# Five more Strassen steps at new places, SiLU in one instruction, and the opening's squares in PSUM

## The chip, the cores and the metric

The kernel runs on one core of a Trainium2 chip. The metric is the device time of one execution in microseconds (us), lower is better; several executions are timed and their median is given. Engines are named as the profile names them: PE is TensorE (PEld its weight loads), DVE is VectorE, ACT is ScalarE, POOL is GpSimd, SP is SyncE, which here only issues transfers.

## The reference

One decoder block in float32 on 256 tokens of width 4096: an RMSNorm, a wide projection, two mixer branches, gates, an output projection with a residual, and a final RMSNorm.

```python
h = rmsnorm(x, norm_w)
proj = einsum('bsd,de->bse', h, w_in)                  # 4096 -> 20480
u_p, z_p, u_c, b_c, c_c, z_c, g_logit = split(proj)    # 6 of width 2048, one of 8192
y_pool = causal_multiscale_pool(u_p, pool_w, pool_scale) * silu(z_p)
y_conv = causal_gated_shortconv(u_c, b_c, c_c, conv_w, conv_b) * silu(z_c)
br = einsum('bsnc,ncd->bsnd', stack(y_pool, y_conv), w_branch)
merged = sum(sigmoid(g_logit + gate_b) * br)           # over the two branches
x = x + einsum('bsd,de->bse', merged, w_out)
return rmsnorm(x, final_norm_w)
```

SiLU is z times its sigmoid. Nearly all the arithmetic is in the three large products (w_in, w_branch, w_out).

## The kernel before

**Units and steps.** The products are cut into units of 1024 output columns, named after what they compute: `cu0 cc0 cz0 cb0 cu1 cc1 cz1 cb1` (convolution branch), `pz0 pu0 pz1 pu1` (pooling branch), `g0_0 g1_0 ... g1_3` (gates), `b0_0 ... b1_3` (branch products), `o0 ... o3` (output). A unit has 16 steps (a branch unit 8). A step takes 256 rows of weights, loads them into one of four `raw` buffers (SP, the queue of `load`, L90), splits each float into a high and a low part in the `ring` buffer (high by ACT, L72; low by a subtraction on DVE, L75), and multiplies: each product of two floats is three matmuls of 128x512 (L1297): high by high, high by low, low by high.

**Two kinds of step.** A plain step ("P") makes 2 token halves x 2 column halves x 2 row halves x 3 = 24 matmuls. A Strassen step ("S") makes seven products in place of eight, so 21 matmuls, and pays for it with sums on DVE: two of the weights' blocks are combined (`W<-raw`, `raw<-raw,W`) and there are three parts to split, so DVE has six instructions where a P step has two. The sum of two of its weight blocks is made in DRAM: SP copies one block to `sum_d` (L1252), POOL adds the other to it with an accumulating transfer (`move_add`, L97), and SP loads the sum. `PLACES` and `OUT` name, for each unit, the step numbers (0 to 15) that are Strassen steps. The others are P. There are 216 S steps.

**Order.** Every engine runs its instructions in the order in which the program writes them. The program walks through PE's steps; after each group of matmuls `pump` writes the preparation of up to three steps ahead, as far as the ring has room, and once every six matmuls `tick` writes the next item of a queue: the epilogue of the unit just finished (one item in the queue is an action, `None` is a pause of one tick) and the filling of the standing operands. The epilogues of the z units (`cz0 cz1 pz0 pz1`) use `sigmoid_mul`:

```python
def sigmoid_mul():
    return gap(4) + [lambda: act(E, R, AF.Sigmoid)] + gap(1) + [lambda: mul(R, R, E)]
```

**The standing operands of the output units.** The products of the branch units, gated and merged, are transposed on PE in each b1 unit's epilogue (`transposes`, L519), copied to `Y`, stored to DRAM (`m_d`) and fetched again by SP into one of two staging tiles, `sa` and `sb`; from there they are split into `arena`. An operand of an S step needs sums first (`sums_s`, four DVE instructions `sa<-...`). `queue_fills` queues these fills in the order in which o0 will use them, that is, in the order that `OUT[0]` gives. The last b1 unit's epilogue lies in the first steps of o0: there DVE multiplies by the gates (`R<-R,E`) and adds the other branch (`R<-R,Y`) for each token half, and PE transposes R right after step 4 has begun.

**The opening.** In the first unit (all P steps) x is split as well, and its squares are summed for the norm, `square(c)` after the preparation of steps 2 to 9: ACT squares into the one tile `W`, DVE adds it to `sq` (the tile `sa`), twice per step. At step 10 PE sums over the partitions (L1086), ACT and DVE make the reciprocal root (`mean`, `rin`, `diag`), and at step 11 PE spreads it (L1094).

Of the kernel before, what the change touches and what calls it, by code (L numbers as in the profile page):

```python
# [29 lines left out]
AF = mybir.ActivationFunctionType  # L30
# [3 lines left out]
T = 256  # L34
# [23 lines left out]
def hybrid_block(ctx: ExitStack, tc: tile.TileContext, x, x_t, norm_t, w_first, w_in, pool_w, pool_scale,  # L58
# [12 lines left out]
    def act(dst, src, func=AF.Copy, **kw):  # L71
        return pin(nc.scalar.activation(dst, src, func, **kw))  # L72

    def tt(dst, a, b, op):
        return pin(nc.vector.tensor_tensor(out=dst, in0=a, in1=b, op=op))  # L75

    def mul(dst, a, b):
        return tt(dst, a, b, ALU.mult)

    def add(dst, a, b):  # L80
        return tt(dst, a, b, ALU.add)
# [23 lines left out]
    def sb(name, shape, dt=F32):  # L105
        return const.tile(shape, dt, name=name)
# [4 lines left out]
    R = sb("R", [P, 2, NU])  # L111
    E = sb("E", [P, 2, NU])
    W = sb("W", [P, NH])
# [45 lines left out]
    def xc(a, b=None):  # L159

        q = flat(xhome[a // 4])[:, a % 4 * 2 * T:((b or a + 1) - 1) % 4 * 2 * T + 2 * T]
        return q if b else q.rearrange("p (k c) -> p k c", k=2)
# [269 lines left out]
    SHARED = [("F", t, n) for t in range(2) for n in range(2)]  # L432
# [5 lines left out]
    def shared(i):  # L438
        return PF[i]
# [71 lines left out]
    def transposes(src, done):  # L511

        items = []
        for j in range(4):
            def f(j=j):
                for i in range(2):
                    for t in range(2):
                        c = (2 * j + i) * P
                        pin(nc.tensor.transpose(shared(j)[:, i * T + t * P:i * T + (t + 1) * P],  # L519
                                                src[:, t, c:c + P], ident))  # L520
                done(j)
            items.append(f)
        return items
# [16 lines left out]
    def gap(n):  # L540
        return [None] * n

    def sigmoid_mul():
        return gap(4) + [lambda: act(E, R, AF.Sigmoid)] + gap(1) + [lambda: mul(R, R, E)]

    units = []

# [61 lines left out]
    def at_places(at):  # L609
        n = NP_X + NS_X  # L610
        ps, ss = list(range(n - len(at))), list(range(n - len(at), n))
        return [("S", ss.pop(0)) if i in at else ("P", ps.pop(0)) for i in range(n)]
# [159 lines left out]
    def band_sums(st):  # L772
        c = st.band
        for b in range(8):
            g = b // 4
            o = shared(b // 2)[:, (b % 2) * T:(b % 2 + 1) * T]
            cs = slice(b * P, (b + 1) * P)
            bands, edge = upper["bands"], upper["edge"]
            pin(nc.tensor.matmul(o, st.h[:, 0, cs], bands[:, g], start=True, stop=False))  # L779
            pin(nc.tensor.matmul(o, st.l[:, 0, cs], bands[:, g], start=False, stop=False))  # L780
            pin(nc.tensor.matmul(o[:, P:T], st.h[:, 1, cs], edge[:, g], start=False, stop=False))
            pin(nc.tensor.matmul(o[:, P:T], st.l[:, 1, cs], edge[:, g], start=False, stop=True))
        rg.release(st.block, 16)
        e = chan(E)
        for i in range(2):
            w = WINDOWS[2 * c + i]
            for j in (2 * i, 2 * i + 1):
                act(e[:, 2 * j:2 * j + 2], bankview(j), scale=1.0 / w)
                mul(e[:, 2 * j:2 * j + 2, 0:w - 1], bankview(j)[:, :, 0:w - 1],
                    ic[:, None, 0:w - 1].to_broadcast([P, 2, w - 1]))  # L790
            st.unit.flags[f"pooled{i}"] = True

    def mix(st):
        g = st.g
        for t in range(2):
            o = shared(2 * g + t)
            ts = slice(t * P, (t + 1) * P)
            for k in range(4):
                for i, (a, b) in enumerate(((st.ah, st.h), (st.ah, st.l), (st.al, st.h))):
                    pin(nc.tensor.matmul(o, a[:, k, ts], b[:, k], start=(k, i) == (0, 0), stop=(k, i) == (3, 2)))  # L800
        rg.release(st.bw, 16)
        rg.release(st.ba, 8)
        cs = slice(g * NH, (g + 1) * NH)
        for t in range(2):
            mul(R[:, t, cs], shared(2 * g + t), Y[:, t, cs])
        if g == 1:
            c = st.c

            def copy(j):
                act(chan(E)[:, 2 * j:2 * j + 2], bankview(j))  # L810
            queue.extend(gap(3) + transposes(R, copy) + [e_done(2, 1), lambda: put(y_d[0, c], chan(E), QUEUE[9]), e_done(8)])
# [37 lines left out]
    merged = {}  # L849


    OUT = ((6, 7, 9, 11, 12, 13, 15), (2, 4, 5, 7, 8, 10, 11, 15), (2, 3, 4, 6, 10, 11, 12, 13), (1, 3, 5, 7, 9, 10, 12))

    def out_unit(c):
        cs = slice(c * NU, (c + 1) * NU)
# [11 lines left out]
        def src(i):  # L867
            return wout[c, i]
        seq = at_places(OUT[c])
        units.append(Unit(f"o{c}", src, seq, m_ops, epi, before=start))  # L870
# [82 lines left out]
    now, filled, units_done = [0], [0], [False]  # L953
# [115 lines left out]
    sq = sa.rearrange("p o c -> p (o c)")  # L1069

    def square(c):

        src = xc(2 * c, 2 * c + 2)
        if c == 0:
            act(sq, src, AF.Square)
        else:
            for n in range(2):
                act(W, src[:, n * 2 * T:(n + 1) * 2 * T], AF.Square)
                add(sq[:, n * 2 * T:(n + 1) * 2 * T], sq[:, n * 2 * T:(n + 1) * 2 * T], W)
        if c == 7:  # L1080
            for n in (2 * T, T):
                add(sq[:, 0:n], sq[:, 0:n], sq[:, n:2 * n])
# [119 lines left out]
    loaded = [s for s in steps if s.src is not None]  # L1202
    for i, s in enumerate(loaded):
        s.load_index = i
    state = dict(limit=0, nl=0, np=0, micros=None, prepared=0, now=0, mm=0)
    queue = deque()

    def issue_load(s):
# [94 lines left out]
    def after_group(u, b):  # L1303
        if b[0] == "E" and u is not last:
            if u.closed(b):
                evacuate(u, *b[1:])
        while state["mm"] >= TICK:
            state["mm"] -= TICK
            tick()
        state["limit"] = state["now"] + min(AHEAD, state["now"] + 1)  # L1310
        pump()
# [5 lines left out]
    def order_of(seq):  # L1317
        return [i for _, i in seq]

    def queue_fills():  # L1320
# [6 lines left out]
        def from_y(n, o, i, ready=None):  # L1327
            later(o, y_d[n, i // 4][:, i % 4].rearrange("p k t -> p (k t)"), place_of(o),
                  ready or (lambda: n == 0 or units_done[0]))

        def from_m(o, i):
            c = i // 4
            if c < 3:
                later(o, m_d[c][:, i % 4].rearrange("p k t -> p (k t)"), place_of(o),
                      lambda: c in merged and now[0] >= merged[c])
            else:
                def src():
                    return chan(Y)[:, 2 * (i % 4):2 * (i % 4) + 2].rearrange("p k (t c) -> p k t c", t=2)
                fills.append(Direct(o, src, place_of(o), lambda: 3 in merged))
# [4 lines left out]
        for n in DIRECT_LAST:  # L1344
            for i in range(NP_Y[n], ny):
                from_y(n, y_last[n][i], i, lambda: all(o.ready for q in y_ops for o in q))
        for i in order_of(at_places(OUT[0])):
            from_m(m_ops[i], i)

    def run_step(u, st):  # L1350
        if st.kind == "B":
            band_sums(st)
            state["mm"] += 10
            after_group(u, ("F", 0, 0))
            return
        if st.kind == "M":
            mix(st)
            state["mm"] += 24
            after_group(u, ("F", 0, 0))
            return  # L1360
        for f in st.first:
            f()
        while not st.op.ready:
            pop_fill(True)
        assert st.kind != "S" or st.op.kind == "S" or st.op.more
        gs = st.groups()
        for i, g in enumerate(gs):
            multiply(u, st, g)
            if i == len(gs) - 1:
                st.op.left -= 1  # L1370

            if st is not steps[0] or i >= len(gs) // 2 - 1:
                after_group(u, g[0])
            if st is steps[0] and i == len(gs) // 2 - 1:
                warm_up(WARM_2)
# [213 lines left out]
```

## Time and profile before

| | |
|---|---|
| median of 3 timed runs | 2369.02 us (2366.8 to 2370.43) |
| the profiled execution: device time | 2372.13 us |
| the profiled execution: span, first to last instruction | 2370.4 us |
| busy in that span: PE / DVE / ACT / POOL | 2350.2 / 2165.5 / 1448.8 / 250.8 us |
| matmuls of 128x512 at L1297 | 7497 in `sums`, 2556 in `shared` |
| HBM traffic | 324 GB/s over the span |

The profile is of one execution. A line of a timeline gives the start and the duration in us, the engine, the source line, the operation, output<-inputs, the shapes, how many instructions are merged in the line, and in brackets how long the engine had been idle before it and what ended that. A line of groups gives the count, then busy us and mean ns of one after the bar, then the idle time before. `SPq` is SP's queue, `PEld` weight loads. Busy matmuls overlap by a part of their length, so the distance of their starts is shorter than the duration of one.

### The profile page before, as it was taken

The numbers are of one execution on the slowest core, as the hardware profiler recorded it, in microseconds if no ns is written. First come the engines' busy times: TensorE is split into PE (matmuls) and PEld (weight loads), VectorE is DVE, ScalarE is ACT, GpSimd is POOL, SyncE is SP. The second block draws the span as 40 slices with busy tenths as digits, with TensorE's granted clock in tenths as the row PEclk, the third lists the DMA queues.
The fourth block names the chain that finished last, engine by engine and source line by source line (L and its number), as shares of the span: only waits on it lengthen the run. The fifth ranks groups of instructions, "written<-read, shape, count | busy, mean of one in ns | idle before, by whom it ended". The sixth has DMA issues, their size and how long they took to land.

```text
span 2370.4 us, 29327 instructions
## 1 busy us (share of the span) xinstructions
PE 2350.2 (99%) x10456; PEld 1943.0 (82%) x10456; DVE 2165.5 (91%) x2345; ACT 1448.8 (61%) x1708; POOL 250.8 (11%) x336
## 2 busy tenths in 40 slices
PE   9999999999999999999999999999999999999998
PEld 7788888888888888888888888888888888788886
DVE  7999999989889979989999999989899898798988
ACT  7655665656556656566665666666565556566555
POOL 0000111010012011110111111100000000111110
PEclk9999999999999999999999999999999999999999
DMA  9777998897998788789999999999988788799886
GB/s 337 228 252 240 299 304 263 280 288 219 299 303 276 244 269 285 227 283 278 306 305 293 307 299 309 276 295 296 305 288 270 269 289 282 243 272 330 270 284 245
DMA packets 178708, 664.06 MB, mean 280 GB/s; under 512 B 19952, under 2 KB 20208, under 8 KB 145024
## 3 DMA queue, kind: packets, MB, share of 16 engines
q1 hardware_dynamic: 135472, 549.28, 63.1%
q0 software_dynamic: 42656, 111.82, 24.1%
q8 instruction: 82, 1.34, 0.2%
q10 hardware_dynamic: 432, 1.07, 0.1%
q14 instruction: 66, 0.54, 0.1%
HBM read 629.26 MB, written 138.74 MB: 324 GB/s over the span
## 4 chain that ended last, share of the span: by engine, by line
PE 95%; DVE 2%; ACT 1%; DMA 1%; issue 1%; SPq 0%; DVEq 0%; ACTq 0%
PE sums L1297 68%; PE shared L1297 25%; DVE ring L75 1%; PE shared L800 1%; PE shared L519 1%; ACT ring L72 1%; DVE R L75 0%; DMA raw<-in_w_in_dram 0%; DMA E<-z_d 0%; ACT arena L72 0%; DVE sa L75 0%; PE shared L779 0%; SPq L90 0%; DVE Y L75 0%; DVE arena L87 0%
## 5 line engine op out<-in xcount | busy, mean ns | idle before, releaser
L1297 PE MATMUL sums<-ring,arena 128*128 128x512 f32 x7497 | 1778.7, 390 | 0.6 <-DVE ring L75 0.4
L1297 PEld LDWEIGHTS sums<-ring,arena 128*128 128x128 f32 x7497 | 1404.9, 188 | 294.3 <-DVE ring L75 2.0
L72 ACT ACTIVATE ring<-raw 128x1024 fp32r<-128x1024 f32 (+2 forms) x1118 | 1118.7, 1053 | 642.8 <-DVE raw L75 424.7
L75 DVE TENSOR_TENSOR ring<-raw,ring 128x1024 fp32r<-128x1024 f32 (+2 forms) x1118 | 1340.4, 1223 | 116.5 <-ACT ring L72 113.7
L1297 PE MATMUL shared<-ring,arena 128*128 128x512 f32 x2556 | 645.7, 389 | 0.8 <-DVE Y L87 0.6
L1297 PEld LDWEIGHTS shared<-ring,arena 128*128 128x128 f32 x2556 | 479.4, 188 | 101.4 <-issue 1.0
L75 DVE TENSOR_TENSOR raw<-raw,W 128x1024 f32<-128x1024 f32 x216 | 264.5, 1225 | 7.0
L97 POOL DMA_DIRECT2D sum_d<-in_w_in_dram x166 | 140.3, 858 | 1222.5 <-DMA sum_d<-in_w_in_dram 1180.0
L72 ACT ACTIVATE ring<-W 128x512 fp32r<-128x512 f32 x216 | 135.9, 629 | 93.6 <-DVE W L75 83.1
L75 DVE TENSOR_TENSOR W<-raw 128x512 f32<-128x512 f32 x216 | 148.3, 687 | 5.2 <-DMA raw<-sum_d 5.1
L75 DVE TENSOR_TENSOR ring<-W,ring 128x512 fp32r<-128x512 f32 x216 | 148.3, 687 | 0.0
L75 DVE TENSOR_TENSOR R<-R,E 128x1024 f32<-128x1024 f32 (+1 forms) x49 | 77.3, 1592 | 10.3 <-DMA E<-z_d 7.3
L72 ACT ACTIVATE arena<-sa 128x512 fp32r<-128x512 f32 (+2 forms) x50 | 26.2, 556 | 78.5 <-DVE sa L75 71.1
L75 DVE TENSOR_TENSOR R<-R,shared 128x512 f32<-128x512 f32 x87 | 59.6, 685 | 4.6 <-ACT R L72 2.1
L72 ACT ACTIVATE E<-sums,rin 128x512 f32<-128x512 f32 x76 | 48.9, 681 | 9.8 <-PE sums L1297 9.8
L97 POOL DMA_DIRECT2D sum_d<-in_w_out_dram x30 | 25.6, 855 | 232.4 <-DMA sum_d<-in_w_out_dram 232.3
L97 POOL DMA_DIRECT2D sum_d<-in_w_branch_dram x20 | 16.7, 836 | 174.6 <-DMA sum_d<-in_w_branch_dram 151.8
L75 DVE TENSOR_TENSOR arena<-sa,arena 128x512 fp32r<-128x512 f32 (+2 forms) x50 | 28.6, 600 | 5.4 <-ACT arena L72 5.3
L519 PE MATMUL shared<-ident,R 128*128 128x128 f32 x160 | 24.6, 287 | 5.6 <-DVE R L75 5.6
L519 PEld LDWEIGHTS shared<-ident,R 128*128 128x128 f32 x160 | 20.6, 148 | 10.8 <-DVE R L75 6.8
L75 DVE TENSOR_TENSOR sa<-sa 128x128 f32<-128x128 f32 (+1 forms) x74 | 18.9, 295 | 8.7 <-DMA sa<-m_d 7.6
L72 ACT ACTIVATE E<-sums 128x512 f32<-128x512 f32 x40 | 22.1, 590 | 7.0 <-PE sums L1297 6.8
(144 smaller groups left out, 488.8 us busy)
## 6 DMA issues: line engine op xcount, KB each, us to landing
raw<-in_w_in_dram SPq DMA_DIRECT2D x152, 1024.0 KB, 8.2
raw<-in_w_in_dram SPq DMA_DIRECT2D x166, 768.0 KB, 7.0
raw<-sum_d SPq DMA_DIRECT2D x216, 256.0 KB, 7.4
raw<-in_w_branch_dram SPq DMA_DIRECT2D x44, 1024.0 KB, 6.7
sum_d<-in_w_in_dram SPq DMA_DIRECT2D x166, 256.0 KB, 8.7
sum_d<-in_w_in_dram POOLq DMA_DIRECT2D x166, 256.0 KB, 8.2
raw<-in_w_out_dram SPq DMA_DIRECT2D x34, 1024.0 KB, 8.1
raw<-in_w_out_dram SPq DMA_DIRECT2D x30, 768.0 KB, 7.3
```

The costliest lines, as they stand in the source:

```text
L72: return pin(nc.scalar.activation(dst, src, func, **kw))
L75: return pin(nc.vector.tensor_tensor(out=dst, in0=a, in1=b, op=op))
L97: return pin(nc.gpsimd.dma_start(dst, src, accum_op=ALU.add))
L519: pin(nc.tensor.transpose(shared(j)[:, i * T + t * P:i * T + (t + 1) * P], src[:, t, c:c + P], ident))
L800: pin(nc.tensor.matmul(o, a[:, k, ts], b[:, k], start=(k, i) == (0, 0), stop=(k, i) == (3, 2)))
L1297: pin(nc.tensor.matmul(ps, lhs, rhs, start=n == 0, stop=n == u.total[b] - 1))
```

## The change

Three things change. The places of the Strassen steps: five more in all (cb1, pu0, pu1, g1_1, o1 and o2 get one more, cz1 has one fewer), and in pz1, g0_0, g1_0, o0 and some of the former the same number stands elsewhere. `sigmoid_mul` becomes one ACT instruction, `Silu`, in place in `R`, with the DVE product gone; the number of ticks stays seven. And `square` writes into two PSUM banks (`shared(0)`, `shared(1)`) instead of into `W` twice; the two adds come after both squares.

```diff
@@ sigmoid_mul
-        return gap(4) + [lambda: act(E, R, AF.Sigmoid)] + gap(1) + [lambda: mul(R, R, E)]
+        return gap(4) + [lambda: act(R, R, AF.Silu), None, None]
@@ PLACES (two of ten changed lines)
-        "pu1": (4, 5, 7, 9, 10, 12, 13, 14),
+        "pu1": (2, 4, 5, 8, 9, 10, 12, 14, 15),
-        "g1_1": (4, 5, 6, 7, 8, 10, 12, 13, 15),
+        "g1_1": (3, 5, 6, 7, 8, 10, 12, 13, 14, 15),
@@ OUT
-    OUT = ((6, 7, 9, 11, 12, 13, 15), (2, 4, 5, 7, 8, 10, 11, 15), (2, 3, 4, 6, 10, 11, 12, 13), (1, 3, 5, 7, 9, 10, 12))
+    OUT = ((5, 6, 10, 11, 13, 14, 15), (2, 4, 5, 7, 8, 10, 11, 12, 15), (2, 3, 4, 6, 10, 11, 12, 13, 15), (1, 3, 5, 7, 9, 10, 12))
@@ square
             for n in range(2):
-                act(W, src[:, n * 2 * T:(n + 1) * 2 * T], AF.Square)
-                add(sq[:, n * 2 * T:(n + 1) * 2 * T], sq[:, n * 2 * T:(n + 1) * 2 * T], W)
+                act(shared(n), src[:, n * 2 * T:(n + 1) * 2 * T], AF.Square)
+            for n in range(2):
+                add(sq[:, n * 2 * T:(n + 1) * 2 * T], shared(n), sq[:, n * 2 * T:(n + 1) * 2 * T])
```

The remaining lines of the diff keep the name of the running unit and assert, as the program is written, that no transpose is written into the `shared` banks while that unit's S steps use them. A row below is a source line, an operation, output<-inputs and a shape; x2 means twice in a row.

The first place is ACT in the opening, from the preparation of step 3 to that of step 5 (`ring<-raw` is the split of the weights, `arena<-E` that of x, the rest are squares). Before:

```order
L72 ACTIVATE ring<-raw 128x1024 x2
L72 ACTIVATE W<-R 128x512 x2
L72 ACTIVATE arena<-E,par_n 128x256 x2
L72 ACTIVATE ring<-raw 128x1024 x2
L72 ACTIVATE W<-E 128x512 x2
```

Now:

```order
L72 ACTIVATE ring<-raw 128x1024 x2
L72 ACTIVATE shared_81<-R 128x512
L72 ACTIVATE shared_82<-R 128x512
L72 ACTIVATE arena<-E,par_n 128x256 x2
L72 ACTIVATE ring<-raw 128x1024 x2
L72 ACTIVATE shared_81<-E 128x512
L72 ACTIVATE shared_82<-E 128x512
```

Nothing moved past anything else; the two squares of a step now have a buffer each, so the second one no longer has the DVE add of the first between it and its predecessor.

The second place is DVE in the first steps of o0, around the gating of the last branch unit (`sa<-sa` are the sums of a Strassen operand fetched from `m_d`, `arena<-sa` its split, `ring` and `W` belong to the weights of o0). Before:

```order
L75 TENSOR_TENSOR ring<-raw,ring 128x1024 x2
L75 TENSOR_TENSOR sa<-sa 128x128 x4
L75 TENSOR_TENSOR ring<-raw,ring 128x1024
L75 TENSOR_TENSOR R<-R,E 128x1024
L75 TENSOR_TENSOR R<-R,Y 128x1024
L75 TENSOR_TENSOR arena<-sa,arena 128x512 x2
L75 TENSOR_TENSOR ring<-raw,ring 128x1024
L75 TENSOR_TENSOR R<-R,E 128x1024
L75 TENSOR_TENSOR R<-R,Y 128x1024
```

Now:

```order
L75 TENSOR_TENSOR ring<-raw,ring 128x1024 x3
L75 TENSOR_TENSOR sa<-sa 128x128 x4
L75 TENSOR_TENSOR arena<-sa,arena 128x512 x2
L75 TENSOR_TENSOR W<-raw 128x512
L75 TENSOR_TENSOR ring<-raw,ring 128x3x512
L75 TENSOR_TENSOR R<-R,E 128x1024
L75 TENSOR_TENSOR R<-R,Y 128x1024
L75 TENSOR_TENSOR raw<-raw,W 128x2x512
L75 TENSOR_TENSOR R<-R,E 128x1024
L75 TENSOR_TENSOR R<-R,Y 128x1024
```

The sums still stand ahead of both gatings; the split and the first part of step 5, now a Strassen step, came between them, and two `ring` subtractions of step 5 went.

The third place is SP's queue at the same time, from the load of o0's step 5 on. Before:

```order
L90 DMA raw<-in_w_out_dram 128x2048
L90 DMA raw<-in_w_out_dram 128x1536
L90 DMA raw<-sum_d 128x512
L1252 DMA sum_d<-in_w_out_dram 128x512
L90 DMA sa<-m_d 128x512
L90 DMA raw<-in_w_out_dram 128x1536
```

Now:

```order
L90 DMA raw<-in_w_out_dram 128x1536
L90 DMA raw<-sum_d 128x512
L1254 DMA sum_d<-in_w_out_dram 128x512
L90 DMA sa<-m_d 128x512
L90 DMA raw<-in_w_out_dram 128x1536
```

The first row of each is the load of step 5. The fetch of the operand into `sa` stood behind the loads of steps 5 and 6 and now stands behind step 5's alone, one load earlier.

More of the change, by code (lines that the diff above doesn't have):

```diff
@@ L515, in f @@
             def f(j=j):
+                assert state["unit"] is None or not any(state["unit"].seen.get(b) for b in SHARED)
                 for i in range(2):
@@ L1204, in hybrid_block @@
         s.load_index = i
-    state = dict(limit=0, nl=0, np=0, micros=None, prepared=0, now=0, mm=0)
+    state = dict(limit=0, nl=0, np=0, micros=None, prepared=0, now=0, mm=0, unit=None)
     queue = deque()
@@ L1350, in run_step @@
     def run_step(u, st):
+        state["unit"] = u
         if st.kind == "B":
```

12 rows, old and new, of the table PLACES are left out of this document.

## The prediction

> **What bounds the kernel.** I read the page's busy times first, then PE's waits, then the timeline at each of them, then the windows of the units that change.
>
> ```profile
> PE 2350.2 (99%) x10456; PEld 1943.0 (82%) x10456; DVE 2165.5 (91%) x2345; ACT 1448.8 (61%) x1708; POOL 250.8 (11%) x336
> ```
>
> PE is the bound, busy 99% of the span. DVE, at 91%, comes close behind, so a change that moves work from PE to DVE has to be checked place by place. PE's waits, longest in total first (us, times, longest):
>
> ```profile
> PE shared L519 <- DVE R L75: 5.6, 2, 4.1
> PE shared L1094 <- DVE diag L1090: 1.6, 1, 1.6
> PE sums L1297 <- DVE ring L75: 0.4, 1, 0.4
> ...
> PE shared L1297 <- DVE ring L75: 0.2, 1, 0.2
> ```
>
> Two waits matter: for a gated R before transposes, and for the norm in the opening. For weights PE hardly waits (the two rows with `ring`: 0.4 in the opening, 0.2 in pu1). So time falls by fewer matmuls or by these two waits, and rises only where DVE comes too late.
>
> **Fewer matmuls.** The opening shows PE's pace:
>
> ```profile
> 17.61 43.59 PE L1297 MATMUL sums<-ring,arena 128*128 128x512 f32 x191 [0.36 <-DVE ring L75]
> 61.40 5.73 PE L1297 MATMUL sums<-ring,arena 128*128 128x512 f32 x24
> 68.72 0.49 PE L1094 MATMUL shared<-diag,ones 128*128 128x128 f32 x2 [1.59 <-DVE diag L1090]
> ```
>
> 43.59/191 = 0.228 us for one matmul. Five S steps for P steps leave out 5 x 3 = 15 matmuls: **-3.4 us**, all on the path, if DVE keeps up.
>
> **The squares.** ACT and DVE in the opening, between two steps:
>
> ```profile
> 20.79 0.61 ACT L72 ACTIVATE W<-R 128x512 f32<-128x512 f32 x1
> 22.97 0.63 ACT L72 ACTIVATE W<-R 128x512 f32<-128x512 f32 x1 [1.56 <-DVE sa L75]
> 23.64 0.69 DVE L75 TENSOR_TENSOR sa<-sa,W 128x512 f32<-128x512 f32 x1 [0.70 <-ACT W L72]
> 25.39 2.36 DVE L75 TENSOR_TENSOR ring<-raw,ring 128x1024 fp32r<-128x1024 f32 x2 [0.27 <-ACT ring L72]
> 26.20 0.62 ACT L72 ACTIVATE W<-E 128x512 f32<-128x512 f32 x1
> 67.09 0.15 DVE L1062 TENSOR_SCALAR mean<-shared 128x2 f32<-128x2 f32 x1
> ```
>
> ACT's second square waits 1.56 for DVE to have read W; DVE then waits 0.70 for that square and 0.27 for ACT's next split. The round takes 26.20 - 20.79 = 5.41 us, just PE's pace of 24 x 0.228 = 5.47, so the pair never gets ahead. With two buffers DVE's 0.97 of waiting goes, seven times over: 6.8 us. DVE reaches `mean` at 67.09, although PE had begun the next step, behind the sums of squares, at 61.40: there are 5.7 us to win, and only the last part counts. PE could have started L1094 at 61.40 + 24 x 0.228 = 66.87 and started at 68.72, 1.85 late. Both 6.8 and 5.7 exceed it, so the whole goes: **-1.8**. No row shows ACT writing PSUM or a square read from there; the nearest are 0.62 (to SBUF) for the one, and for the other a DVE add of 128x512 with a PSUM input, 685 ns, against 689 with W:
>
> ```profile
> L75 DVE TENSOR_TENSOR R<-R,shared 128x512 f32<-128x512 f32 x87 | 59.6, 685 | 4.6 <-ACT R L72 2.1
> ```
>
> Bounds 0 and -1.85; below nothing only if PSUM cost 0.5 more per square, which that row excludes for DVE. The banks are idle in the opening (PE's sums use another).
>
> **SiLU.** Four DVE products of 2.29 us go, 9.2 us of DVE; ACT's instruction stays.
>
> ```profile
> L75 DVE TENSOR_TENSOR R<-R,E 128x2048 f32<-128x2048 f32 x17 | 38.9, 2291 | 8.6 <-DMA E<-z_d 7.3 <-ACT E L72 0.8
> L72 ACT ACTIVATE E<-R 128x2048 f32<-128x2048 f32 x4 | 7.7, 1915 | 5.3 <-DMA R<-E 5.3
> L72 ACT ACT_TABLE_LOAD x4 | 5.1, 1283 | 1.3 <-PEq L1575 1.2
> ```
>
> No row has Silu: its neighbours of that size are all near 1.91, which I take. In the new order one more table load stands ahead of the first gate's sigmoid (1.28 us of ACT, 61% busy). Both lie beside PE: nothing by themselves; they pay for S steps.
>
> **What the S steps cost DVE.** The forms, with the busy time of all after the bar:
>
> ```profile
> L75 DVE TENSOR_TENSOR ring<-raw,ring 128x1024 fp32r<-128x1024 f32 x678 | 801.5, 1222 | 69.0 <-ACT ring L72 66.5 <-PE sums L1297 1.3
> L75 DVE TENSOR_TENSOR ring<-raw,ring 128x1536 fp32r<-128x1536 f32 x216 | 379.0, 1755 | 45.6 <-ACT ring L72 45.2
> L75 DVE TENSOR_TENSOR raw<-raw,W 128x1024 f32<-128x1024 f32 x216 | 264.5, 1225 | 7.0
> L75 DVE TENSOR_TENSOR ring<-raw,ring 128x512 fp32r<-128x512 f32 x220 | 150.9, 686 | 0.8 <-ACT ring L72 0.8
> ```
>
> S: 1.76 + 1.23 + 1.18 (801.5/678) + three of 128x512 at 0.69 = 6.2. P: 2 x 1.18 = 2.4. So an added S step gives DVE 3.8 more in a unit that is 0.7 shorter: it needs 4.5 us of DVE's idle time there. The units that gain one (window, then busy us of PE, PEld, DVE, ACT, POOL), in order cb1, pu0, pu1, g1_1, g0_2 for comparison, o1, o2:
>
> ```profile
> 591.50:673.10 81.60, 81.60 (x361) 67.59 (x361) 72.47 (x72) 51.97 (x58) 8.86 (x11) 1.00 0.94 304
> 757.80:839.40 81.60, 81.60 (x362) 67.57 (x361) 76.64 (x77) 49.96 (x55) 5.77 (x7) 1.00 0.82 276
> 936.80:1019.10 82.30, 82.13 (x361) 67.41 (x360) 76.18 (x83) 48.99 (x55) 13.81 (x19) 1.00 0.79 250
> 1277.80:1358.80 81.00, 81.00 (x359) 67.05 (x359) 75.28 (x76) 50.88 (x56) 10.02 (x12) 1.00 0.97 303
> 1358.80:1439.20 80.40, 80.40 (x356) 66.46 (x355) 78.14 (x79) 52.36 (x58) 10.07 (x12) 1.00 0.98 301
> 2114.20:2195.80 81.60, 81.60 (x362) 67.57 (x361) 71.76 (x72) 50.51 (x58) 11.32 (x14) 1.00 1.02 324
> 2195.80:2277.40 81.60, 81.60 (x362) 67.57 (x361) 77.03 (x78) 49.03 (x58) 9.44 (x11) 1.00 0.88 273
> ```
>
> DVE idles 9.1, 5.0, 6.1, 5.7, (2.3), 9.8 and 4.6 us. SiLU adds 2.3 in cb1, pu0 and pu1. After 4.5 there remain 6.9, 2.8, 3.9, 1.2, 5.3 and 0.1. g0_2 has ten S steps as g1_1 will have, lives on 2.3, and PE is busy in all of it; so these numbers suffice if the idle time lies ahead of the need. In pu1 it does: the added S step stands at step 2, and
>
> ```profile
> 960.95 1.92 ACT L72 ACTIVATE E<-R 128x2048 f32<-128x2048 f32 x1 [4.90 <-DMA R<-E]
> 963.84 2.36 DVE L75 TENSOR_TENSOR ring<-raw,ring 128x1024 fp32r<-128x1024 f32 x2 [5.01 <-ACT ring L72]
> ```
>
> ACT waits there for a transfer with the splits queued behind it, and DVE idles 5.0 for these; 3.8 of work fits in. I count pu1's 0.2 of waiting for weights as won, **-0.2**. In g1_1 and o2 the added step comes last or last but one; behind o2 the next unit has slack, in g1_1 two S steps now end the unit. There I take a wait of **+0.5** (bounds 0, and 4.5 - 1.2 = 3.3, were none of its idle time in time). The sums in DRAM add five copies and five loads on SP and five accumulations on POOL. Of what 216 of them cost now the profile shows
>
> ```profile
> DVE W L75 <- DMA raw<-sum_d: 5.1, 3, 4.2
> ```
>
> 5.1/216 = 0.02 of DVE for one: 0 (bounds 0 and the longest, 4.2, if one lands late; cover is DVE's lead over PE).
>
> **The wait ahead of o0's transposes**, the 4.1 of PE's list. PE, DVE, SP, and the window with its granted clock (the 1.00 and 0.51 before the last two columns):
>
> ```profile
> 2050.47 1.75 PE L519 MATMUL shared<-ident,R 128*128 128x128 f32 x7 [4.14 <-DVE R L75]
> 2022.52 1.29 DVE L75 TENSOR_TENSOR arena<-sa,arena 128x512 fp32r<-128x512 f32 x2
> 2031.99 2.35 DVE L75 TENSOR_TENSOR ring<-raw,ring 128x1024 fp32r<-128x1024 f32 x2
> 2038.87 1.02 DVE L75 TENSOR_TENSOR sa<-sa 128x128 f32<-128x128 f32 x4 [4.53 <-DMA sa<-m_d]
> 2049.19 1.22 DVE L75 TENSOR_TENSOR R<-R,Y 128x1024 f32<-128x1024 f32 x1
> 2026.78 0.58 SPq L90 DMA_DIRECT2D sa<-m_d  x1
> 2049.50:2056.40 6.90, 5.93 (x22) 5.24 (x23) 6.87 (x8) 3.05 (x5) 0.81 (x1) 0.51 0.54 188
> ```
>
> PE wants the gated R at 2046.3. DVE stood from 2034.34 for an operand fetch issued at 2026.78 and landed at 2038.87 (12.1 later), and finished the second `R<-R,Y` at 2050.41, 11.5 after that. In the new order SP issues this fetch one load earlier: it then waits only for its staging tile, which DVE frees at 2022.52 + 1.29 = 2023.81, 3.0 earlier. With the same 12.1 it lands at 2035.9. What DVE has between the sums and the second `R<-R,Y` then is 1.0 + 1.3 + 0.7 + 1.8 + 5 x 1.2 = 10.8, with one short wait for ACT again some 11.5: done at 2047.4, PE waits 1.1. **-3.0** (bounds: 0, if it lands as late as now; -4.1, if it lands before DVE is free at 2034.34). And PE's clock: at 0.51 for 6.9 us after the wait, of which PE worked 5.93: lost 0.49 x 5.93 = 2.9. The shorter of PE's two waits on this line, 5.6 - 4.1 = 1.5, has no such window. A wait of 1.1 is nearest to that one: **-2.9** (bounds 0 and -2.9). Where between 1.5 and 4.1 the clock falls no row tells. The Trainium skill has it under "TensorE: Matmul & The Clock Gate", What's actually happening: the gate halves the clock after an idle window of about 3.4 us that runs free of the program. By it a remaining wait of up to 3.4 keeps the clock, and a wait of 4.1 loses it in some executions and not in others; the trace has one such case only, in agreement.
>
> **Sum.** -3.4 - 1.8 - 0.2 + 0.5 - 3.0 - 2.9 = -10.8 against the profiled execution's own 2372.1: 2361. That execution is 3.1 above the median 2369.0. If the 3.1 is the lost clock (2.9), the median has 10.8 - 2.9 = 7.9 to win: 2361 again; if not, 2369 - 10.8 = 2358. I say **2359.5**. What is late next is DVE behind o0's step 5 and in g1_1.
>
> **Rivals.**
> - *The fetch stays late* (0.2). The new fetch is behind step 5's loads, which are now an S step's, and lands near 2038.9 as before; then o0's wait and the clock stay, and -4.9 is left: 2364. For it: landing took 12.1. Against it: it waits for two transfers fewer.
> - *S steps come too late* (0.15). Waits for `ring` in g1_1 (3.3), o2 (4.4, if its 4.5 are not there in time) or pz1, where S moves to step 4, take back half of the gain: about 2366, within 0.2% of before. For it: 1.2 and 0.1 us of idle time. Against it: g0_2.
> - *DVE is the bound* (0.05), the other side. If what PE saves only turns into waits for DVE, the span follows DVE's work: 5 x 3.8 - 9.2 = +9.8, so 2379. It begins to decide when DVE's idle time in a unit falls below zero and no unit after it has any to give. Against it: 2370.4 - 2165.5 = 205 us of idle time, and a PE that waits 0.4 for weights.
> - That the change doesn't do what it says is excluded: the new order has 221 S steps, no `R<-R,E` behind the four, and two PSUM squares.
>
> **Numbers.** My case has 0.6: 2359.5, own range 2355 to 2362.5: low, no wait left in o0 or g1_1 (-10.8 - 1.1 - 0.5 = -12.4, so 2356.6) and 1.6 of the 2.2 by which the fastest run shown beats the median; high, one term of 3 missing. With the fetch late and S steps late the range is 2355 to 2366.5; DVE as the bound and the worst of the third case stay out. Runs of this kernel tell some 0.2% (4.7 us) from no change. Faster by over 0.2%, under 2364.3: my 0.6 and the larger half of the second case and a little of the third, 0.76; within: 0.19; slower: 0.05.
>
> **What would show it.** Right: L1094 without a wait; 15 matmuls fewer at the same 0.228; `sa<-sa` in o0 with a wait under 2 and the transposes behind it with one under 1.5, granted clock 1.00 there; PE's waits for `ring` under 1 us in all. Wrong: a wait of PE for `ring` at the end of g1_1 or in o2 of several us, Silu longer than 1.91, or ACT's table load landing where DVE has nothing else. What would upset the number most is a new wait of over 3 us before any transposes, since it brings the half clock with it.

## The result

| | before | after |
|---|---|---|
| median of 4 runs each | 2368.82 us (2366.8 to 2370.43) | 2355.91 us (2355.73 to 2357.04) |
| ratio, 95% interval | 1 | 0.9945 (0.9933 to 0.9958) |
| profiled execution: device time / span | 2372.13 / 2370.4 us | 2357.04 / 2355.3 us |
| half clock of PE behind o0's transposes (profiled execution) | 6.83 us | none |

The changed kernel is 0.55% faster: 12.9 us between the medians, 15.1 between the profiled executions. I had forecast 2359.5, so 3.6 more came than I said. (The profiled execution of before is 3.3 above its median, that of after 1.1; hence the two differences.)

The page's busy times and PE's whole list of waits (us, times, longest), after:

```profile
PE 2342.3 (99%) x10441; PEld 1939.2 (82%) x10441; DVE 2172.5 (92%) x2361; ACT 1460.5 (62%) x1719; POOL 253.4 (11%) x341
PE shared L1050 <- DVE rout L1055: 1.1, 1, 1.1
PE shared L520 <- DVE R L75: 1.1, 1, 1.1
PE sums L1299 <- ACT R L72: 0.4, 1, 0.4
```

There are 15 matmuls fewer (10456 to 10441). The waits for `diag` and for `ring` are gone. The 1.1 for `rout`, in the final norm, stood in the list before as well and stays. Of the two waits ahead of transposes (5.6) only the shorter is left, at 688 us, with 1.1. A wait of 0.4 is new: at o0's start PE waits for ACT to empty a bank, because ACT has the split of a standing operand, now needed earlier, ahead of that in its queue.

Where the time went is seen best from the starts of the units (first matmul, us), read from PE's timeline in both profiled executions:

| first matmul of | before | after | gained so far |
|---|---|---|---|
| cc0 | 96.6 | 94.5 | 2.1 |
| cb0 | 263.4 | 260.3 | 3.1 |
| cb1 | 591.5 | 588.5 | 3.0 |
| pz1 | 839.4 | 834.5 | 4.9 |
| g0_0 | 1019.1 | 1012.9 | 6.2 |
| g0_2 | 1358.8 | 1352.0 | 6.8 |
| o0 | 2022.9 | 2015.9 | 7.0 |
| o1 | 2114.2 | 2100.7 | 13.5 |
| o3 | 2277.4 | 2262.5 | 14.9 |

The opening gave 2.1 and cz0 another 0.9; of the six units with one more S step five gave 0.5 to 0.7 each (cb1, pu0, g1_1, o1, o2) and pu1 1.4, cz1 with one fewer took 0.4; o0, which has no matmul fewer, gave 6.5. Single executions differ too: with the old squares the first unit, from its first matmul to that of cc0, took 90.6 to 91.6 us in the four traces there are (before and three of the runs below), with the new ones 88.9 to 89.8 in ten. So the opening's 2.1 is 1.7 between the means, 91.1 and 89.4.

**The opening** after, ACT and DVE for the same round of squares as shown of before, then PE at L1096 (before: L1094), where `diag` is needed:

```profile
20.53 1.10 ACT L72 ACTIVATE shared<-R 128x512 f32<-128x512 f32 x2
21.99 1.28 DVE L75 TENSOR_TENSOR sa<-shared,sa 128x512 f32<-128x512 f32 x2
24.27 1.10 ACT L72 ACTIVATE shared<-E 128x512 f32<-128x512 f32 x2
61.36 0.16 DVE L1063 TENSOR_SCALAR mean<-shared 128x2 f32<-128x2 f32 x1 [0.74 <-PE shared L1088]
66.75 0.38 PE L1096 MATMUL shared<-diag,ones 128*128 128x128 f32 x2
```

The two squares now stand back to back, with no idle time in brackets; the round takes 24.27 - 20.53 = 3.74 us where it took 5.41, against PE's 5.47. So DVE runs ahead: it reaches `mean` at 61.36, 5.7 earlier, and waits there for PE rather than PE for it. L1096 has no wait.

**o0** after: SP's fetch of the operand, DVE's sums on it and its gating, PE's transposes, and the window that answers to the one at clock 0.51.

```profile
2019.85 0.34 SPq L90 DMA_DIRECT2D sa<-m_d  x1
2027.38 1.01 DVE L75 TENSOR_TENSOR sa<-sa 128x128 f32<-128x128 f32 x4
2037.45 1.23 DVE L75 TENSOR_TENSOR R<-R,Y 128x1024 f32<-128x1024 f32 x1
2039.75 1.03 PE L520 MATMUL shared<-ident,R 128*128 128x128 f32 x8
2039.50:2046.40 6.90, 6.90 (x40) 5.90 (x39) 6.83 (x11) 4.43 (x8) 0.00 (x0) 1.00 0.52 190
```

DVE's sums wait for nothing (before: 4.53), R is done at 2038.7, 1.1 ahead of PE, the eight transposes come without a wait, and in 6.90 us PE does 40 instructions at clock 1.00 where it had done 22 at 0.51.

**SiLU**, the group on ACT with Sigmoid and Silu together (eight and four of them), and the table loads:

```profile
L72 ACT ACTIVATE R<-R 128x2048 f32<-128x2048 f32 x12 | 22.9, 1908 | 0.5 <-DMA R<-E 0.5
L72 ACT ACT_TABLE_LOAD x5 | 6.4, 1283 | 1.3 <-PEq L1578 1.2
```

The mean of 1908 ns says that Silu costs what Sigmoid does (1904 of the eight before), and there is one table load more, both as forecast.

### The profile page after: what moved, and what is told of

Same layout as the page of the kernel before. It is cut to its first block, busy times and chain, and to the rows that moved or that the text cites. A ratio compares the mean times of both kernels' runs of the same rounds, so it can differ in the third digit from the quotient of the medians.

```text
span 2355.3 us, 29359 instructions
## 1 busy us (share of the span) xinstructions
PE 2342.3 (99%) x10441; PEld 1939.2 (82%) x10441; DVE 2172.5 (92%) x2361; ACT 1460.5 (62%) x1719; POOL 253.4 (11%) x341
## 4 chain that ended last, share of the span: by engine, by line
PE 96%; DMA 2%; DVE 1%; issue 0%; ACT 0%; SPq 0%; DVEq 0%; ACTq 0%
PE sums L1299 69%; PE shared L1299 25%; PE shared L801 1%; PE shared L520 1%; DMA sa<-m_d 0%; DMA raw<-in_w_in_dram 0%; DMA E<-z_d 0%; DVE ring L75 0%; DMA sb<-m_d 0%; DVE R L75 0%; ACT ring L72 0%; SPq L90 0%; PE shared L780 0%; DVE arena L75 0%; DVE Y L75 0%
## 5 line engine op out<-in xcount | busy, mean ns | idle before, releaser
L1299 PE MATMUL sums<-ring,arena 128*128 128x512 f32 x7419 | 1760.7, 390 | 0.5 <-ACT R L72 0.4
L1299 PEld LDWEIGHTS sums<-ring,arena 128*128 128x128 f32 x7419 | 1390.3, 188 | 289.7 <-ACT R L72 0.8
L1299 PE MATMUL shared<-ring,arena 128*128 128x512 f32 x2604 | 656.8, 389 | 0.0
L1299 PEld LDWEIGHTS shared<-ring,arena 128*128 128x128 f32 x2604 | 488.6, 188 | 101.5
L75 DVE TENSOR_TENSOR raw<-raw,W 128x1024 f32<-128x1024 f32 x221 | 270.7, 1225 | 7.1
L75 DVE TENSOR_TENSOR R<-R,E 128x1024 f32<-128x1024 f32 (+1 forms) x45 | 68.0, 1530 | 9.5 <-DMA E<-z_d 6.9
L72 ACT ACTIVATE R<-R 128x2048 f32<-128x2048 f32 x12 | 22.9, 1908 | 0.5 <-DMA R<-E 0.5
```

The costliest lines, as they stand in the source:

```text
L1299: pin(nc.tensor.matmul(ps, lhs, rhs, start=n == 0, stop=n == u.total[b] - 1))
```

## The experiments

### Each part alone

Four kernels carry one part of the change on top of the kernel before. The first has the two PSUM banks for the squares.

```diff
-                act(W, src[:, n * 2 * T:(n + 1) * 2 * T], AF.Square)
-                add(sq[...], sq[...], W)
+                act(shared(n), src[:, n * 2 * T:(n + 1) * 2 * T], AF.Square)
+            for n in range(2):
+                add(sq[...], shared(n), sq[...])
```

> The kernel before with the opening's squares in two PSUM banks, nothing else. Theory A: the edit takes away the wait of 1.59 at L1094 (cc0 starts 2.1 earlier, as after) and, because DVE leaves the opening with up to 7 us more lead, also the short wait of 0.8 at about 211 us in cz0: -2.9 us in all (2366.0 against 2368.8), and units behind cb0 keep the pace of before. Rival B: only the wait at L1094 goes and the lead is used up at once: -1.9. Rival C: later waits of before give it back: 0.

Measured: 2365.88 us, ratio 0.9986 (0.9978 to 0.9995), 3.6 us under the 2369.43 of before in the same series. In its trace cc0 starts 2.2 earlier and cb0 3.2, as in after. PE's timeline in cz0, of before, shows what the second step of that was:

```profile
211.64 0.69 PE L1297 MATMUL shared<-ring,arena 128*128 128x512 f32 x2 [0.63 <-DVE Y L87]
```

DVE was 0.63 late there with the taps of the convolution; with the lead from the opening it isn't, and the line has no counterpart in this run. Theory A holds; the interval is wide enough to hold B (-1.9) too, so it is the traces that decide between them: cz0 takes 84.4 us in all four with the old squares and 83.6 in nine of the ten with the new. The tenth, the run with four sums below, has the wait of 0.6 for `Y` again, so the lead doesn't always suffice.

The second has only o0's new places:

```diff
-    OUT = ((6, 7, 9, 11, 12, 13, 15), ...
+    OUT = ((5, 6, 10, 11, 13, 14, 15), ...
```

> The kernel before with only o0's Strassen steps at their new places (same number of them). Theory A: this alone removes o0's wait of 4.14 for the gated R and the half clock behind it (2.9), less a new wait of some 0.5 at o0's start: o0 6.5 us shorter, 2362.3, clock 1.00 all through o0; the operand's fetch lands within 5 us of its issue and not after 12. Rival B: the fetch lands late as before, since the short landing came from what the other edits did to the traffic: 0 to -1. Rival C: the wait goes but the clock drop stays, so that it has another cause than the wait: -3.6.

Measured: 2364.16 us, ratio 0.9978 (0.9969 to 0.9988), 5.3 us under before. PE's transposes in o0 come without a wait, and the clock stays at 1.00. In the two traces o0 is 6.8 us shorter. So this one line of numbers carries o0's part of the gain by itself. One thing was not as expected: the fetch took 6.9 us to land, not under 5, and that was soon enough.

The third has only Silu:

```diff
-        return gap(4) + [lambda: act(E, R, AF.Sigmoid)] + gap(1) + [lambda: mul(R, R, E)]
+        return gap(4) + [lambda: act(R, R, AF.Silu), None, None]
```

> The kernel before with z times its sigmoid by one ScalarE instruction, nothing else. Theory A: 9.2 us of DVE go, but PE did not wait for DVE in those units except some tenths (cz1 and pu1 0.3 each), so the time moves by 0 to -0.6 (2368.2 to 2368.8). Rival B: DVE is the bound in the units behind the z units and its saving counts: -2 to -9. Rival C: the extra table load or a longer Silu delays ACT's splits: +1.3 or more.

Measured: 2369.59 us, ratio 0.9995 (0.9986 to 1.0004): no change, as theory A has it. 9.2 us of DVE's work gone, and nothing of it on the path.

The fourth has the new places of all units except o0, and nothing else of the change:

> The new places of the Strassen steps in all units except o0 (five more steps, 15 matmuls fewer), with the old squares, the old sigmoid and product, and o0's old places. Theory A: -3.4 for the matmuls and some -1 for waits of some tenths that go, less a late step in pz0 or pu0, where DVE has 2.3 us less than with Silu and the last step of pz0 had 0.1 to spare: in all -2.5 (2366.3), with o0's wait of about 4 still there. Rival B: Silu's relief is not needed for them: -5 (2363.8). Rival C: without it the five steps come late by as much as they save: 0 or slower.

Measured: 2363.2 us, ratio 0.9976 (0.9967 to 0.9985), -6.2. The ratio's interval holds rival B's -5 and not A's -2.5, and the trace shows two reasons. Up to o0's start it gains 4.0 us, and cb1, pu0, pu1 and g1_1 give their 0.5 to 1.4 each without Silu. And in o0, which it does not touch, it gains 3.2, because the transposes wait only 1.99 in this execution and the clock holds. The lines of this run in o0, PE and DVE:

```profile
2044.26 0.98 PE L520 MATMUL shared<-ident,R 128*128 128x128 f32 x7 [1.99 <-DVE R L75]
2032.66 1.02 DVE L75 TENSOR_TENSOR sa<-sa 128x128 f32<-128x128 f32 x4 [2.91 <-DMA sa<-m_d]
```

So o0's wait is not fixed by the order in o0 alone. What it follows is the time from issue to landing of that one fetch, 256 KB into `sa`. In order: before, this run, o0's places alone, after.

```profile
DMA to landing us min/median/max: 12.0/12.0/12.0
DMA to landing us min/median/max: 10.4/10.4/10.4
DMA to landing us min/median/max: 6.9/6.9/6.9
DMA to landing us min/median/max: 4.2/4.2/4.2
```

The waits that go with these are 4.14, 1.99, none and none. In all four SP issues the fetch 3.3 to 3.9 us after o0's start. What differs is what was issued just before: in before a step's 1024 KB at 2017.4, two gate tiles of 512 KB at 2021, then at 2025.4 a step's 768 KB and two blocks of 256 KB, and the fetch behind them at 2026.78; in after SP's last issue ahead of the fetch was at 2014.44, 5.4 us earlier. The windows between issue and landing, of before and after (DMA share and GB/s are the last two columns):

```profile
2026.78:2038.78 12.00, 12.00 (x54) 9.95 (x53) 5.46 (x9) 4.01 (x5) 0.57 (x1) 1.00 1.03 369
2019.85:2024.06 4.21, 4.21 (x20) 3.51 (x19) 4.18 (x9) 3.00 (x5) 0.89 (x2) 1.00 1.08 320
```

The DMA engines are full in both. 12.0 x 369 is 4.4 MB moved before the fetch was in, 4.21 x 320 is 1.3 MB. When the fetch was issued, 3840, 3840, 2304 and 2048 KB of earlier transfers had not landed, in the order above (some of them partly moved). In each of the four traces all of these landed before it and nothing issued later did. So the fetch lands when the transfers ahead of it are through; that is read from four traces, no run varied this backlog alone.

By medians the four parts sum to 3.6 + 5.3 - 0.2 + 6.2 = 14.9 us, against 12.9 above and 14.3 in a later series for the whole. They need not add up exactly: the steps and o0's places both take away part of the same wait.

### Does Silu pay for the steps?

The changed kernel with the old `sigmoid_mul`:

> The changed kernel with the old sigmoid and product in place of Silu: DVE has 9.2 us more to do, everything else is as after. Theory A (from the run with the new steps alone, where the added steps of cb1, pu0 and pu1 came in time without Silu): +0 to +0.4, some 2356, no wait of PE for ring in pu0 or pu1, lowest lead there 1.7 instead of 3.4. Rival B (my prediction's own sentence that the instruction pays for the steps): DVE comes late in pz0, pu0 or pu1 and the time rises by 2 to 7 us, with waits for ring there.

Measured: 2356.07 us, ratio to before 0.9942 (0.9930 to 0.9955). After itself, run again as a control:

> The changed kernel once more, to compare the one above with it on the same chip: 2355.9, spread below 1.5 us, no half clock inside.

Measured: 2355.97 us (2355.75 to 2356.53), 0.9943 (0.9930 to 0.9955). The two are the same. Silu is worth nothing in this kernel, alone or with the steps. PE's waits in the run with the sigmoid:

```profile
PE shared L520 <- DVE R L75: 0.8, 1, 0.8
PE sums L1299 <- ACT ring L72: 0.7, 1, 0.7
```

The rest of the list is 1.1 for `rout` and 0.2 for ACT's `arena`; there is none for DVE's `ring`. DVE's smallest lead over PE in pu0, behind the first steps (from the end of a step's first subtraction on DVE to PE's first matmul of the step, worked out from the two timelines), is 1.4 us, against 3.4 with Silu: less, and enough. Rival B falls.

### What makes the clock fall

Three kernels put idle DVE work (E added to itself, read by nothing) between the two gatings of the last branch unit, so that PE waits for R by a chosen time. The first two differ in the number of sums, 3 and 4:

```diff
+            ... [add(E[:, 0], E[:, 0], E[:, 0]) for _ in range(3 if c == 3 else 0)] ...   # behind the first gating
```

> The changed kernel with three idle DVE sums (E plus E, 128x1024, 1.2 us each, read by nothing) between the two gatings ahead of o0's transposes, to make a wait of known length there: DVE finishes R 1.1 before PE wants it, so PE waits 3.6 - 1.1 = 2.5. Theory A (the clock is judged in fixed periods of 3.41 us that start at any phase, and a period with mostly idle PE halves the next): a wait of 2.5 seldom fills enough of a period, so the time is +2.5 in most executions (2358.4), clock 1.00, and in a few +4. Rival B (a wait must itself exceed about 3.4): +2.5 in all. Rival C (the clock falls for any wait over 2): +2.5 and 1.7 more in all, 2360.

Measured: 2359.22 us (2358.58 to 2361.12), 3.3 over after's; a wait of 2.27 in the trace and clock 1.00. Three of the five runs lie between 2358.6 and 2359.2, two at 2360.5 and 2361.1, and the mean granted clock of these two is 0.998, of the others 0.999. That fits theory A; the third decimal of a mean, which moves by 0.001 in runs without a drop too, does not prove it.

> The same with four such sums: PE waits 4.9 - 1.1 = 3.8, as long as the waits in the kernel before. Theory A: one or two periods of 3.41 us at half clock follow in nearly all executions, each costing up to 1.7: +5.5 to +7.2, 2361.4 to 2363.1, scattering by some us from run to run as the kernel before does. Rival B (the drop of before came from something else in o0 than the wait): +3.8, 2359.7, no half clock.

Measured: 2362.57 us (2361.4 to 2364.47), 6.7 over after's, with a wait of 4.06 and 6.83 us at half clock in the trace: before's loss, made on purpose. Rival B falls; the wait causes the drop.

The third makes two waits out of one, by gating the second token half in two column halves with three and two sums ahead of them:

> The changed kernel with o0's second gating done in two column halves and idle DVE sums (read by nothing) ahead of them, three and two of 1.2 us, so that PE has two separate waits of about 1.5 before its two pairs of transposes, with six matmuls (1.4) between them. Neither wait is longer than those that kept the clock in the kernel before. Theory A (a fixed period of 3.41 us counts, and one in which PE multiplies for less than about half of it halves the next, as two short waits did at 749 and at 1681 us in the run with three more steps): half clock for one period or two in most executions, +2.9 for the waits and +1.7 or more, 2360.5. Rival B (a single wait of some 3 us is needed): +2.9, 2358.8, clock 1.00.

Measured: 2359.79 us (2359.07 to 2361.15). The waits were 1.28 and 1.24 and the clock stayed; four of the five runs have 0.999. As expected by B, against A. But B had been contradicted by then. The run with more steps (next section) lost the clock twice with no single wait over 1.6. What separates most of the cases is seen when windows are laid on the clock's own grid. In every trace here the clock's changes lie whole multiples of 3.413 us apart (half-rate stretches of 3.41 or 6.83; full-rate stretches such as 2037.76 and 2341.54, 597 and 686 times 3.413). Windows of one such period, PE's busy time after the comma and the granted clock before the last two columns; first three periods that were followed by half clock (Silu alone; 4 sums; more steps), then four that were not (3 sums; two waits; more steps; 4 sums at the wait near 688):

```profile
2044.88:2048.29 3.41, 0.88 (x5) 0.45 (x3) 3.38 (x5) 0.00 (x0) 0.00 (x0) 1.00 0.03 7
2039.71:2043.12 3.41, 1.08 (x6) 0.61 (x4) 3.38 (x4) 0.60 (x1) 0.00 (x0) 1.00 0.00 0
749.09:752.50 3.41, 1.66 (x7) 0.81 (x6) 3.41 (x5) 2.54 (x3) 0.00 (x0) 1.00 1.00 197
2036.78:2040.19 3.41, 1.95 (x10) 1.32 (x8) 3.38 (x4) 1.52 (x2) 0.00 (x0) 1.00 0.01 2
2041.78:2045.19 3.41, 2.17 (x14) 1.67 (x13) 3.38 (x6) 0.90 (x2) 0.00 (x0) 1.00 0.00 0
1677.51:1680.92 3.41, 1.99 (x8) 1.00 (x6) 3.34 (x7) 1.11 (x2) 0.00 (x0) 1.00 0.80 318
688.03:691.44 3.41, 1.58 (x9) 1.40 (x10) 3.41 (x4) 0.00 (x0) 0.15 (x1) 1.00 0.74 107
```

Over all the traces, every full-rate period with 1.4 us of work or less was followed by half clock, and none with 1.8 or more. Between these the busy time alone does not decide: the two drops of the run with more steps came behind 1.66 and 1.62, both of matmuls alone, while the last line, with most of a wait of 2.06 and four transposes in it, kept the clock at 1.58. It also matters how a wait lies: the 2.27 of the run with 3 sums was split between two periods. At the time I drew the line between 1.66 and 1.95. Two waits of 1.25 with 2.5 of work between them can't bring a period under it; two of 2.5 should:

```diff
-                for k, h in ((3, slice(0, NH)), (2, slice(NH, NU))):
+                for k, h in ((4, slice(0, NH)), (3, slice(NH, NU))):
```

> As the kernel with two waits before the pairs of transposes, with one more idle sum of 1.2 ahead of each half (four and three): two waits of about 2.5, with 2.6 of PE's work between them. Theory A, sharpened by the runs so far: a period of 3.41 in which PE is busy 1.66 or less halves the clock, one with 1.95 or more does not, and transposes count as busy. With two waits of 2.5 some period has at most 1.7 of work at nearly any phase: half clock for one period or more in most executions, +5.8 for the waits and about +1.7, 2363.5, with a spread of 2 us. Rival B (one wait of 3 us or more is needed): 2361.8 and clock 1.00.

Measured: 2362.83 us (2361.97 to 2363.95). The waits were 2.67 and 1.26 (PE works longer between them at half clock, and that hides the rest of the second), and a period at half clock follows the first, with no wait as long as 3 us. The mean clock is 0.998 or 0.997 in all nine runs (0.999 in all five of the control). Its period ahead of the drop, the one at half clock, and the next:

```profile
2039.00:2042.41 3.41, 0.90 (x8) 0.91 (x9) 3.38 (x4) 0.32 (x1) 0.00 (x0) 1.00 0.00 0
2042.41:2045.82 3.41, 2.82 (x8) 1.74 (x6) 3.31 (x5) 0.77 (x2) 0.00 (x0) 0.50 0.00 0
2045.82:2049.23 3.41, 2.74 (x16) 2.40 (x17) 3.41 (x5) 1.60 (x3) 0.00 (x0) 1.00 0.00 0
```

So B falls, and this drop is as sharpened A has it; one wait of 2.67 in one period was enough for it. That short waits add up is shown by the run with more steps alone. The time would not have told it: it lies between A's 2363.5 and B's 2361.8. The trace does.

### More of the same

Three more S steps where DVE had a lead, and the transposes of cb1 one pause later:

```diff
-        "pz0": (4, 6, 7, 8, 10, 11, 12, 14, 15),
-        "g0_3": (2, 4, 5, 8, 9, 10, 12, 13, 15),
-        "g1_3": (3, 4, 6, 9, 11, 13, 14),
-    OUT = (..., (1, 3, 5, 7, 9, 10, 12))
-    ... e_done()] + gap(3) + transposes(R, gate)
+        "pz0": (5, 6, 7, 8, 10, 11, 12, 14, 15),
+        "g0_3": (2, 4, 5, 8, 9, 10, 12, 13, 14, 15),
+        "g1_3": (3, 4, 6, 9, 11, 13, 14, 15),
+    OUT = (..., (1, 3, 5, 7, 9, 10, 11, 12))
+    ... e_done()] + gap(3 + c) + transposes(R, gate)
```

> The changed kernel with three more Strassen steps where DVE's lead was above 3.5 us (g0_3 step 14, g1_3 step 15, o3 step 11) and with cb1's transposes one pause later, behind the wait of 1.1 at 687 us (for that, pz0's first Strassen step goes from 4 to 5). Theory A: 9 matmuls fewer at 0.228 are -2.05, the wait is -1.1: 2352.8. Rival B: DVE's lead of 3.5 to 5 does not carry a step of 4.5, and a wait for ring in g1_3 or b0_0 takes it back: 2355 or more. Rival C: the wait for the gated R only moves to the next pause: -2.05, 2353.9.

Measured: 2366.01 us (2363.8 to 2368.23), 10 us over after. Rival B, and far beyond its number. PE's two longest rows of waits and the two stretches at half clock:

```profile
PE sums L1299 <- DVE ring L75: 4.1, 5, 1.6
PE sums L1299 <- ACT ring L72: 2.5, 3, 1.0
752.50:755.91 3.41, 3.41 (x9) 2.64 (x10) 3.18 (x3) 3.41 (x6) 0.81 (x1) 0.50 0.69 207
1684.34:1687.75 3.41, 3.41 (x10) 2.64 (x9) 3.41 (x5) 3.41 (x6) 0.00 (x0) 0.50 0.84 312
```

pz0 lost 2.8 us and g1_3 9.1, o3 gained 0.4. In pz0 no S step was added, one was only moved from 4 to 5: with a P step at 4 DVE's lead there (measured as above) is 13.0, but the ring cannot carry it on, and at step 6 it is 5.0 where it had been 7.0; the last step's high part, from ACT, then came late by 1.0 and its low part, from DVE, by another 0.75, and that sufficed to halve the clock. In g1_3 the lead at the start is 2.9 in place of 6.6, since g0_3's new step used it up. A lead is not a sum that can be spent anywhere. Which of g0_3's and g1_3's steps did the harm wasn't tried apart.

From this I kept what had worked, o3's step, and took the wait at 688 us in another way:

```diff
-    gap(6) + [lambda: mul(R, R, E), e_done()]
+    gap(6) + [lambda: [mul(R[:, :, h], R[:, :, h], E[:, :, h]) for h in (slice(0, NH), slice(NH, NU))], e_done()]
```

> The changed kernel with one more Strassen step in o3 (step 11, where DVE's lead was 6.0; it was in time in the run with three more steps) and the conv branch's last product R<-R,E in two column halves, so that the first two transposes wait for the first half alone. Theory A: -0.68 for three matmuls and about -1.0 for the wait at 687 us: 2354.2. Rival B: the transposes behind the second half wait instead: -0.7, 2355.2.

Measured: 2356.14 us (2355.54 to 2356.42), against 2355.97 of after beside it: no gain. The wait at 688 is gone from the trace, and PE's last matmuls begin 0.5 earlier than in the control (2343.18 against 2343.68), but the span is 2354.7 against 2354.8. Such tenths are lost among the 0.8 by which runs of one kernel differ. No version that beats after was found.

## Why the prediction was right, and where its steps were wrong

- *Matmuls, -3.4.* Right in size and cause: five units gave 0.5 to 0.7 each, pu1 its share (next but one) and cz1 lost 0.4. The windows of cb1 and g1_1 after, to set against 81.60 and 81.00:

```profile
588.50:669.40 80.90, 80.90 (x358) 67.00 (x357) 73.11 (x74) 52.73 (x58) 8.83 (x11) 1.00 0.93 294
1271.60:1352.00 80.40, 80.40 (x355) 66.44 (x354) 76.45 (x77) 50.18 (x57) 10.89 (x13) 1.00 0.98 300
```

- *g1_1, +0.5.* No wait came; the second row is all PE. It was the cautious end of a bound, and g0_2's row had already said that ten S steps can run without one.
- *pu1, -0.2.* The unit gave 1.4, 0.7 of it matmuls, so this was 0.7. With the old places the unit took 81.6 us in two traces of other runs and 82.9 in a third, with the new ones 80.9 in all: in some executions of the old order PE waits there, and before's was one. What else of its 82.30 went besides the listed wait was not traced.
- *Squares, -1.8.* In the opening this was right: 2.1 in this pair of traces, 1.7 between the means. But another 0.9 came in cz0. The step that failed: "only the last part counts" of DVE's 5.7. The rest is a lead that lasts beyond the unit, and the wait of 0.6 for `Y` fell to it. The list of waits in the prediction leaves that row out without a mark, and the 1.1 for `rout`, though both are longer than the 0.4 that it shows; I had dropped the small waits by their size and not asked what a longer lead of DVE does to them.
- *The wait in o0, -3.0.* The size was nearly right (4.14 went, 0.4 came new), the working wrong. I took the fetch to be issued 3.0 earlier and to take 12.1 as before. Against o0's start it is issued no earlier, 3.9 us behind it in both, since the tile it waits for comes free later in the new order. What changed is the landing, 12.0 to 4.2. My rival with the late fetch rested on the same fixed 12.1; what stood "against it", two transfers fewer ahead, is what shortened the landing.
- *The half clock, -2.9.* Right, and the cause is shown by the run with four sums. What I quoted from the Trainium skill ("TensorE: Matmul & The Clock Gate", What's actually happening), a free-running window of about 3.4 us, agrees with the grid of 3.413 in all traces here. That a whole window must be idle does not: windows with 1.62 and 1.66 us of work lost the clock. My sentence that a wait of up to 3.4 keeps the clock is refuted by the wait of 2.67. It did no harm, because no wait near it was left.
- *SiLU, 0.* Right by itself; wrong in "they pay for S steps". The added steps come in time with the sigmoid too.
- *The sum.* Against its own execution the terms gave -10.8 and the traces show -15.1: 1.3 of the difference is the opening with cz0, 1.2 the units cz1, pu1 and g1_1, 0.6 o0, 0.4 pz0, where the wait at 688 went from 1.42 to 1.06, and the rest tenths. Halfway between the two readings of the median was then too careful.

## What to carry to other kernels

A transfer's landing time is not its own property: before pricing a moved fetch, add up what is issued in the 10 us ahead of it; in the four traces looked at it landed behind all of that. Count PE's idle time per stretch of 3.4 us, not per wait: several short waits close together can halve the clock where one of 2 us doesn't, and then a small delay costs twice. And an engine's lead is bounded by its buffer: work taken off it pays only where its lead was the limit, and work put on it must be placed where the buffer is full.

## What was not expected of the hardware

- PE's clock fell for a period of 3.41 us in every case in which PE was busy for 1.4 us or less of the one before, and in none with 1.8 or more; in between, 1.62 and 1.66 lost it and 1.58 kept it, so there is more to it than the busy time. It rises again behind a period at half clock with 2.82 us of work, and stayed down behind 2.50 (before, 2049.56 to 2052.97) and 2.21. Where between these the limit lies isn't settled.
- Transposes seem to count as work for it: of the 2.17 us in the period 2041.78 to 2045.19 (two waits) at most 1.3 are matmuls of 128x512, the rest transposes, and the clock stayed, while 1.66 of matmuls alone lost it; the period that kept it at 1.58 held four transposes.
- The wait's length does not set how long the half clock lasts: 3.41 us behind a wait of 3.93 (squares alone), 6.83 behind 3.72 (Silu alone) and 4.14. The runs of before scatter by 7 us (2364.66 to 2371.94 in 31), those of after by 1.3. That this comes from the wait's length and from where in a period it begins fits, but single runs without a trace don't show it.
